# Longer down rounds, one PSUM bank for a gate product, and a new order of work behind the attention

## The chip, the core and the metric

The kernel runs on one core of a Trainium2 chip. The metric is the device time in microseconds (us). A core has five engines that run side by side and wait for each other by semaphores: TensorE (PE) multiplies matrices into PSUM, VectorE (DVE) and ScalarE (ACT) work element by element and empty PSUM, GpSimd (POOL) does small vector work and issues some DMAs, and SyncE (SP) issues most of the other DMAs. Each engine works off its own instructions in a fixed order, so an instruction that waits holds up all those behind it on the same engine.

## The reference

A residual stream of 512 tokens by 1024 features goes through two layers: a gated short convolution with a SwiGLU block behind it, then windowed attention with sinks and again a SwiGLU block. Everything is float32.

```python
def swiglu(h, w_gate_up, w_down):
    g, u = jnp.split(h @ w_gate_up, 2, axis=-1)
    return (jax.nn.silu(g) * u) @ w_down          # F = 2816 hidden columns

mix = short_conv_mixer(rmsnorm(h, a_pre_norm[l]), ...)           # layer 0
h = h + rmsnorm(mix, a_post_norm[l])
h = h + rmsnorm(swiglu(rmsnorm(h, ffn_pre_norm[0]), ...), ffn_post_norm[0])
attn = sliding_window_sink_attention(q, k_sh, v_sh, sinks) @ b_w_o[j]   # layer 1
h = h + rmsnorm(attn, b_post_norm[j])
h = h + rmsnorm(swiglu(rmsnorm(h, ffn_pre_norm[1]), ...), ffn_post_norm[1])
```

## The kernel before

**Three matmuls for one.** Every float32 operand is split into a high part (a copy rounded by ACT: `whi`, `xhi`, `ohi`) and a low part (what is left, subtracted by DVE: `wlo`, `xlo`, `olo`). `mm3` (L190 to L193) then issues three matmuls: high times low, high times high, low times high.

**Seven products for eight.** The large products of a SwiGLU block go by Strassen's scheme: 2 by 2 blocks, seven products P1 to P7 instead of eight. That needs sums of weight blocks. They are made in DRAM: class `Sums` lists DMA copies and accumulating DMAs (`hsum`), `sum_on` begins them at places that the table `BEGIN` names and moves them on a step at each place, and `issue` (L535 in the trace) has POOL issue them. An accumulating DMA waits, on POOL, for the copy that it adds to. Where a sum is not made in DRAM, DVE adds the two blocks (L454).

**SwiGLU.** The 2816 hidden columns are 22 tiles of 128. `gate_jobs` makes two hidden tiles (a pair of "row tiles", index `e`) for gate and up at once: seven jobs, one for each product, each 24 matmuls of 256 columns. The products add up along three chains of PSUM banks, X (P1, P6, P7, P4), Z (P5, P3) and Y (P2); `take(p, e)` empties or combines what stands in a bank behind each product, before the next product is added on top. The result is split by `pair_sums` into the factors of the down product, six small steps that are put off ("late") and worked off one for each later job. `ROUNDS` says which hidden tiles form a round of the down product. `down_jobs` makes seven jobs where a round has four tiles, and eleven where it has six; a job brings one 128x1024 weight tile, is prepared three jobs ahead (`LINE_LEAD`) and its products end with DVE (L636) or, in the first round, ACT (L634) adding PSUM to `mix`. The last four tiles are not a round: `close` or the end of the kernel multiplies them directly.

**The seam.** `close` ends a block: for four row tiles of tokens it makes the last part of the product in two halves, `take` (L259) adds it to `mix`, `square_mix` (L264) squares it, `mean` (L293 on DVE, then L297 on POOL, a power of -0.5) makes the norm's factor, `update` (L302) adds to the stream `h`, `square` (L310), `mean2` (L315, then L319 on POOL) and `norm` (L324) make `xn` for the next block. PE then turns `xn` (`turn`, L335): the turn of tokens' tiles 0 and 1 stands on PE between two parts of the last half product, and the last ones among the first gate products. `Ahead.one` splits one weight tile for the next block (L408 on ACT, L413 on DVE). The attention before it is written as a pipeline of ten steps `i` over eight pairs of heads; the string `ORDER` sets what is issued in a step, all engines in one order.

What a pass of the attention's loop and the seam behind it did (`KT` is 8):

```python
                if op in "RH":
                    issue(len(issues) // 2 if op == "R" else len(issues))
            sum_on(f"a{i + 1}")
        ...
        close(rest_w, at, EARLY, res, ahead)
```

Of the kernel before, what the change touches and what calls it, by code (L numbers as in the profile page):

```python
# [12 lines left out]
AF = mybir.ActivationFunctionType  # L13
# [5 lines left out]
S = 512  # L19
KT = D // P  # L20
F = 2816
NF = F // P
ROUNDS = [(0, 6), (6, 10), (10, 14), (14, 18), (18, 22)]

PLAIN = 2

# [1 line left out]

BEGIN = {
# [4 lines left out]
}  # L34


# [8 lines left out]

EARLY_IN, REST_IN = 2, 0
ORDER = (
    "R- T0 g0 S0 O- T1 Q0 M0 Q1 Z0 P0 P1 S1 T2 L0 Q2 L1 G M1 E00 E01 T3 H- Q3 P2 P3 E10 E11 Z1 z0 K W0 L2 L3 N0 W1 W2 N1 W3 g1 z1"
)
STEP = {  # L50
    "S": "scores", "M": "maxima", "E": "exponents", "N": "normalise", "T": "turn", "P": "high",
# [21 lines left out]
def yoco_kernel(  # L73
# [780 lines left out]
        if square:  # L854
            res.square(t)

    def close(ws, x, k0, res, ahead, then=None):


        n = len(x) - k0  # L860

        def part(ps, t, half, ks):
            unit(ps, t, ws[len(ws) // 2 * half :], x, ks, n, k0)

        begun = [bank("pmix", ps_mm) for _ in range(2)]
        for half in range(2):
            part(begun[half], 0, half, range(n - 1))
            ahead.one()
            ahead.one()
        for t in range(NB):  # L870
            for half in range(2):
                if t == 0:
                    ps = begun[half]
                    part(ps, t, half, range(n - 1, n))
                else:
                    ps = bank("pmix", ps_mm)
                    if (t, half) == (NB - 1, 1):
# [74 lines left out]
    def ffn(l, before, ahead, gain, gpres, following):  # L952
# [20 lines left out]
        def gate_jobs(q, factors, out, to, then):  # L973

            sums = sums_of[f"g{l}{q}"]
            a21, a22, a11, a12 = (Raw(b) for b in sums.blocks)
            s1, s3, *rest = (Raw(b) for b in sums.sums)
            raws = {1: [a11], 2: [a12], 5: [s1], 7: [s3], 4: [a22]}  # L980
            if rest:
                raws[6], raws[3] = ([r] for r in rest)
            else:
                raws[6], raws[3] = [a11, s1], [a12, a11]
            chain = {1: "X", 6: "X", 7: "X", 4: "X", 5: "Z", 3: "Z", 2: "Y"}
            pools = {"X": ps_mm, "Y": ps_pt, "Z": ps_sc}
# [8 lines left out]
            def take(p, e):  # L995
                x, y, z = (banks[c][e][:, :256] if c in banks else None for c in "XYZ")
                gr = kept[2]
                g0, g1 = (gr[:, c : c + 256] for c in (e * S, e * S + 256))
                s, u = kept[e][:, :256], kept[e][:, 256:]
                if p in (1, 6):  # L1000
                    nc.scalar.activation(s, x, AF.Copy)  # L1001
                elif p == 2:
                    nc.vector.tensor_tensor(out=g0, in0=y, in1=s, op=ALU.add)
                elif p == 5:
                    nc.scalar.activation(u, z, AF.Copy)
                elif p == 7:
                    nc.vector.tensor_tensor(out=u, in0=x, in1=u, op=ALU.add)
                elif p == 3:
                    nc.vector.tensor_tensor(out=g1, in0=z, in1=s, op=ALU.add)
                else:  # L1010
                    for g, m in ((g0, x), (g1, u)):
                        nc.vector.scalar_tensor_tensor(out=g, in0=m, scalar=-1.0, in1=g,
                                                       op0=ALU.mult, op1=ALU.mult)

            def run(p):
                def products(job):
                    if not kept:
                        kept.extend([slot("st"), slot("st"), wide("gr")])
                    whi, wlo = split[p] if p in split else job.w
                    c = chain[p]  # L1020
                    opened = c not in banks
                    if opened:
                        banks[c] = [bank("g" + c.lower(), pools[c]) for _ in range(2)]
                    for e in range(2):
                        for k in range(4):
                            kk = slice(e * S + k * P, e * S + (k + 1) * P)
                            mm3(banks[c][e][:, :256], whi[:, kk], wlo[:, kk], *factors[p][k],
                                opened and k == 0, k == 3 and p in (2, 3, 4),
                                skip_group_check=True)
                        take(p, e)  # L1030
                return products

            def gate():
                for e in range(2):
                    both = kept[2][:, e * S : (e + 1) * S]
                    nc.scalar.activation(both, both, AF.Silu)

# [407 lines left out]
    with tc.manual_schedule(engines=ALL):  # L1445
        sum_on("a0")
        for i in range(KT + 2):
            for c in ORDER.split():
                if c == "K":
                    if i == 2:  # L1450
                        ks.append(rope_split(rope(pk[1], nc.gpsimd), nc.gpsimd))
                    continue
                late = c.endswith("-")
                op, n = c[0], [int(d) for d in c[1:].rstrip("-")]
                t = i - late
                if op == "g":

                    u = 2 * (t - EARLY - 1) + n[0]
                    if u in (-2, -1, 2, 3):
                        j = u + 2 if u < 0 else u  # L1460
                        early_w.append(split_weights(w_o[j // 2, j % 2], slots=j >= EARLY_IN))
                    continue
                if op in "SMENTPLWO":
                    t -= op in "TPLWO"
                    of = hp
                elif op in "QRH":
                    t += LEAD
                    of = qs
                elif op == "G":
                    t += LEAD + 1  # L1470
                    of = qs
                    if KT <= t < KT + 4:
                        j = t - KT
                        rest_w.append(split_weights(w_o[j // 2, 2 + j % 2], slots=j >= REST_IN))
                else:
                    t = 2 * (t - EARLY - 1) + n.pop(0)
                    of = early
                if 0 <= t < len(of) and not (op in "RH" and t < LEAD - 1):
                    getattr(of[t], STEP[op])(*n)
                if op in "RH":  # L1480
                    issue(len(issues) // 2 if op == "R" else len(issues))
            sum_on(f"a{i + 1}")

        res = Update(mix_o, B_ATT, [G_FPRE[1]])
        res.leaves = True
        res.load()
        ahead = Ahead(first_weights(1))
        close(rest_w, at, EARLY, res, ahead)
    ffn(1, res, ahead, B_FFN[1], [], [])


# [93 lines left out]
```

## Time and profile before

| | |
|---|---|
| time, median of 3 runs | 1027.85 us (1027.74, 1027.85, 1031.52) |
| the profiled execution: its time | 1032.36 us |
| its span, first to last instruction | 1030.6 us |
| granted TensorE clock over the span | 0.997 |
| busy: PE, weight loads, DVE, ACT, POOL | 1019.1, 927.8, 823.2, 577.7, 195.3 us |
| the conv seam (layer 0) | about 160 to 190 us into the span |
| attention, and the seam behind it | about 540 to 660, and 660 to 700 us |

PE is busy in almost every slice, so a saving counts only where PE waits. Time that an engine spends issuing or waiting isn't busy time. In the views, a wait stands in brackets behind the instruction that waited, with what ended it; "x4" is four instructions in one row, and a row with a count gives the time of all of them together.

### The profile page before, as it was taken

How to read it: one execution, taken by the hardware profiler on the slowest of the kernel's cores; microseconds unless marked ns; L12 is line 12 of the kernel's file. 1: busy time of each engine (PE TensorE's matmuls, PEld its weight loads, DVE VectorE, ACT ScalarE, POOL GpSimd, SP SyncE). 2: the span in 40 equal slices, each digit the busy share in tenths (PEclk: the TensorE clock that was granted, in tenths of full speed). 3: DMA queues.
4: the chain of work that ended last, by engine and by line, in shares of the span. 5: the costliest groups of instructions: out<-in, count | busy, mean ns of one | idle time of the engine just before them, and what ended most of it. 6: DMA issues, size and time to landing. Idle time of an engine off the chain costs nothing.

```text
span 1030.6 us, 17465 instructions
## 1 busy us (share of the span) xinstructions
PE 1019.1 (99%) x6648; PEld 927.8 (90%) x6648; DVE 823.2 (80%) x1400; ACT 577.7 (56%) x1035; POOL 195.3 (19%) x259
## 2 busy tenths in 40 slices
PE   9999999999999999999999999989999999999997
PEld 8888888999899898998897888879998999989986
DVE  5766767888688879779869999668886788887786
ACT  7323445865655354656566677667565554645642
POOL 0333033111111111000124653121111010210001
PEclk9999999999999999999999999999999999999999
DMA  9897689459968699778404789865889676988732
GB/s 355 284 261 229 184 254 353 130 169 299 351 229 293 194 314 332 242 232 296 146 21 149 190 273 254 248 223 158 261 287 328 176 252 203 312 296 251 246 136 82
DMA packets 66580, 244.59 MB, mean 237 GB/s; under 512 B 7872, under 2 KB 8384, under 8 KB 54720
## 3 DMA queue, kind: packets, MB, share of 16 engines
q1 hardware_dynamic: 51328, 145.98, 38.4%
q0 software_dynamic: 14592, 96.48, 36.4%
q8 instruction: 52, 0.85, 0.3%
q10 hardware_dynamic: 576, 1.02, 0.3%
q14 instruction: 32, 0.26, 0.1%
HBM read 237.15 MB, written 102.76 MB: 330 GB/s over the span
## 4 chain that ended last, share of the span: by engine, by line
PE 90%; DVE 4%; DMA 3%; ACT 1%; issue 1%; POOL 1%; DVEq 0%; ACTq 0%
PE gx L193 7%; PE gx L192 7%; PE gx L191 7%; PE gz L193 4%; PE gz L192 4%; PE gz L191 4%; PE pcub L192 4%; PE pcub L193 4%; PE pcub L191 4%; PE px L191 4%; PE px L192 4%; PE px L193 4%; PE pmix L192 2%; PE pmix L191 2%; PE pmix L193 2%; DMA hsum<-in_w_gb_dram 2%
## 5 line engine op out<-in xcount | busy, mean ns | idle before, releaser
L467 DVE TENSOR_TENSOR wlo<-raw,whi 128x1024 fp32r<-128x1024 f32 x225 | 275.2, 1227 | 93.3 <-ACT whi L466 93.2
L466 ACT ACTIVATE whi<-raw 128x1024 fp32r<-128x1024 f32 x225 | 234.2, 1049 | 117.5 <-DVE raw L454 20.4
L191 PE MATMUL gx<-xt,whi 128*128 128x256 f32 x480 | 135.8, 283 | 0.0
L192 PE MATMUL gx<-xt,whi 128*128 128x256 f32 x480 | 135.8, 283 | 0.0
L193 PE MATMUL gx<-xt,wlo 128*128 128x256 f32 x480 | 135.8, 283 | 0.0
L191 PEld LDWEIGHTS gx<-xt,whi 128*128 128x128 f32 x480 | 92.2, 192 | 0.0
L192 PEld LDWEIGHTS gx<-xt,whi 128*128 128x128 f32 x480 | 92.2, 192 | 0.0
L193 PEld LDWEIGHTS gx<-xt,wlo 128*128 128x128 f32 x480 | 92.2, 192 | 0.0
L535 POOL DMA_DIRECT2D hsum<-in_w_gb_dram x96 | 63.4, 747 | 143.7 <-ACT whi L466 82.2
L1001 ACT ACTIVATE st<-gx 128x256 f32<-128x256 f32 x80 | 30.6, 385 | 83.5 <-PE gx L193 83.5
L535 POOL DMA_DIRECT2D hsum<-hsum x32 | 25.3, 790 | 262.4 <-ACT whi L466 208.6
L192 PE MATMUL pcub<-xhi,whi 128*128 128x512 f32 x168 | 65.4, 389 | 0.0
L191 PE MATMUL pcub<-xlo,whi 128*128 128x512 f32 x168 | 65.4, 389 | 0.0
L193 PE MATMUL pcub<-xhi,wlo 128*128 128x512 f32 x168 | 65.4, 389 | 0.0
L191 PE MATMUL px<-wlo,ahi 128*128 128x512 f32 x120 | 46.7, 389 | 0.0
L192 PE MATMUL px<-whi,ahi 128*128 128x512 f32 x120 | 46.7, 389 | 0.0
L193 PE MATMUL px<-whi,alo 128*128 128x512 f32 x120 | 46.7, 389 | 0.0
L193 PE MATMUL gx<-xhi,wlo 128*128 128x256 f32 x160 | 45.3, 283 | 0.0
L191 PE MATMUL gy<-xlo,whi 128*128 128x256 f32 x160 | 45.3, 283 | 0.0
L192 PE MATMUL gy<-xhi,whi 128*128 128x256 f32 x160 | 45.3, 283 | 0.0
L193 PE MATMUL gy<-xhi,wlo 128*128 128x256 f32 x160 | 45.3, 283 | 0.0
L191 PE MATMUL gz<-xt,whi 128*128 128x256 f32 x160 | 45.3, 283 | 0.0
(268 smaller groups left out, 3122.5 us busy)
## 6 DMA issues: line engine op xcount, KB each, us to landing
hsum<-in_w_gb_dram POOLq DMA_DIRECT2D x96, 512.0 KB, 7.9
raw<-hsum SPq DMA_DIRECT2D x88, 512.0 KB, 8.2
raw<-in_w_gb_dram SPq DMA_DIRECT2D x60, 512.0 KB, 7.4
hsum<-in_w_dn_dram POOLq DMA_DIRECT2D x36, 512.0 KB, 8.3
raw<-in_w_dn_dram SPq DMA_DIRECT2D x32, 512.0 KB, 7.3
hsum<-hsum POOLq DMA_DIRECT2D x28, 512.0 KB, 5.6
raw<-in_w_in_dram SPq DMA_DIRECT2D x21, 512.0 KB, 7.6
hsum<-in_w_dn_dram POOLq DMA_DIRECT2D x12, 768.0 KB, 12.6
```

The lines of the kernel that those rows point to most:

```text
L191: nc.tensor.matmul(out, whi, xlo, start=start, stop=False, **kw)
L192: nc.tensor.matmul(out, whi, xhi, start=False, stop=False, **kw)
L193: nc.tensor.matmul(out, wlo, xhi, start=False, stop=stop, **kw)
L466: self.begun = nc.scalar.activation(hi[:, :n], raw, AF.Copy)
L467: nc.vector.tensor_tensor(out=lo[:, :n], in0=raw, in1=hi[:, :n].bitcast(F32), op=ALU.subtract)
L535: nc.gpsimd.dma_start(dst, src, max_dma_last_dim=4 * 4 * S, **kw))
L1001: nc.scalar.activation(s, x, AF.Copy)
```

## The change

Three edits.

1. `ROUNDS` has three rounds of six tiles and a last group of four, in place of one round of six, three of four and the four. Each layer has one round fewer; the sums for a round of six are 768 KB to a DMA in place of 512 KB. `BEGIN` follows: `d03` and `d13` are gone, `g09` and `g19` begin at `0p4` and `1p4`.
2. A gate product's two row tiles share one PSUM bank (256 columns each), and `take` runs once behind both, on 512 columns, in place of once behind each on 256.
3. The seam behind the attention. Three of the four `ahead.one()` go into the attention's step `i == KT`, in front of the last `weigh` steps. `res` and `res.load()` are made a little earlier. In the last step (`i == KT + 1`) POOL issues nothing more; the summing of `a10` runs inside `close`, behind row tile 0 (as it already does in the conv seam).

```diff
-ROUNDS = [(0, 6), (6, 10), (10, 14), (14, 18), (18, 22)]
+ROUNDS = [(0, 6), (6, 12), (12, 18), (18, 22)]
...
-    def close(ws, x, k0, res, ahead, then=None):
+    def close(ws, x, k0, res, ahead, then=None, each=2):
...
-            ahead.one()
-            ahead.one()
+            for _ in range(each if half == 0 or each > 1 else 0):
+                ahead.one()
...
                     if opened:
-                        banks[c] = [bank("g" + c.lower(), pools[c]) for _ in range(2)]
+                        banks[c] = bank("g" + c.lower(), pools[c])
                     for e in range(2):
                         for k in range(4):
                             kk = slice(e * S + k * P, e * S + (k + 1) * P)
-                            mm3(banks[c][e][:, :256], whi[:, kk], wlo[:, kk], *factors[p][k],
-                                opened and k == 0, k == 3 and p in (2, 3, 4),
-                                skip_group_check=True)
-                        take(p, e)
+                            mm3(banks[c][:, e * 256 : (e + 1) * 256], whi[:, kk], wlo[:, kk],
+                                *factors[p][k], opened and e == k == 0,
+                                e == 1 and k == 3 and p in (2, 3, 4), skip_group_check=True)
+                    take(p)
...
             def gate():
-                for e in range(2):
-                    both = kept[2][:, e * S : (e + 1) * S]
-                    nc.scalar.activation(both, both, AF.Silu)
+                nc.scalar.activation(kept[2], kept[2], AF.Silu)
...
         for i in range(KT + 2):
+            if i == KT:
+                res = Update(mix_o, B_ATT, [G_FPRE[1]])
+                res.leaves = True
+                ahead = Ahead(first_weights(1))
+            if i == KT + 1:
+                res.load()
             for c in ORDER.split():
+                if c == "A":
+                    if i == KT:
+                        ahead.one()
+                    continue
...
-                if op in "RH":
+                if op in "RH" and i <= KT:
                     issue(len(issues) // 2 if op == "R" else len(issues))
-            sum_on(f"a{i + 1}")
-
-        res = Update(mix_o, B_ATT, [G_FPRE[1]])
-        res.leaves = True
-        res.load()
-        ahead = Ahead(first_weights(1))
-        close(rest_w, at, EARLY, res, ahead)
+            if i <= KT:
+                sum_on(f"a{i + 1}")
+        close(rest_w, at, EARLY, res, ahead, lambda: sum_on(f"a{KT + 2}"), 1)
```

In `ORDER`, `L2 L3 N0 W1` becomes `L2 L3 A A A N0 W1`. `take` keeps its seven cases.

What moves on POOL at the seam behind the attention. `ur` is the norm's factor (L297 for `mean`, L319 for `mean2`), the `hsum<-in_w_dn` rows are the DMAs of the sum for down round 1 of layer 1 (four copies, then two that add); before:

```order
L535 DMA hsum_187<-in_w_gb_dram 64x2048
L535 DMA hsum_208<-in_w_dn_dram 64x2048
L535 DMA hsum_209<-in_w_dn_dram 64x2048
L535 DMA hsum_210<-in_w_dn_dram 64x2048
L535 DMA hsum_211<-in_w_dn_dram 64x2048
L535 DMA hsum_208<-in_w_dn_dram 64x2048
L535 DMA hsum_209<-in_w_dn_dram 64x2048
L297 TENSOR_TENSOR ur_7503<-uv_7502,mhalf 128x1
L319 TENSOR_TENSOR ur_7503<-uv_7502,mhalf 128x1
```

The same place on POOL in the changed kernel:

```order
L535 DMA hsum_183<-in_w_gb_dram 64x2048
L535 DMA hsum_204<-in_w_dn_dram 96x2048
L535 DMA hsum_205<-in_w_dn_dram 96x2048
L535 DMA hsum_206<-in_w_dn_dram 96x2048
L535 DMA hsum_207<-in_w_dn_dram 96x2048
L297 TENSOR_TENSOR ur_7248<-uv_7247,mhalf 128x1
L535 DMA hsum_204<-in_w_dn_dram 96x2048
L535 DMA hsum_205<-in_w_dn_dram 96x2048
L319 TENSOR_TENSOR ur_7248<-uv_7247,mhalf 128x1
```

The two adding DMAs have moved from in front of row tile 0's first factor (L297) to behind it, and now stand in front of its second (L319); the four copies are half as large again.

What moves on DVE at the same seam, from the last steps of the attention (`plo`, `lp`, `olo`) to the first `take` (L259); before:

```order
L1347 TENSOR_TENSOR plo_7432<-pt_7426,phi_7431 128x512
L1347 TENSOR_TENSOR lp_5860<-pt_7445,lp_5859 128x2x128
L1365 TENSOR_TENSOR olo_7497<-po_7467,ohi_7496 128x512
L413 TENSOR_TENSOR wlo_7523<-raw_7507,whi_7522 128x1024
L413 TENSOR_TENSOR wlo_7529<-raw_7509,whi_7528 128x1024
L413 TENSOR_TENSOR wlo_7544<-raw_7526,whi_7543 128x1024
L413 TENSOR_TENSOR wlo_7550<-raw_7532,whi_7549 128x1024
L259 TENSOR_TENSOR mixo_6963<-pmix_7511,mixo_6963 128x512
```

The same place on DVE in the changed kernel:

```order
L1349 TENSOR_TENSOR plo_7295<-pt_7289,phi_7294 128x512
L1349 TENSOR_TENSOR lp_5716<-pt_7308,lp_5715 128x2x128
L413 TENSOR_TENSOR wlo_7340<-raw_7249,whi_7339 128x1024
L413 TENSOR_TENSOR wlo_7346<-raw_7251,whi_7345 128x1024
L413 TENSOR_TENSOR wlo_7352<-raw_7343,whi_7351 128x1024
L1367 TENSOR_TENSOR olo_7380<-po_7330,ohi_7379 128x512
L413 TENSOR_TENSOR wlo_7395<-raw_7349,whi_7394 128x1024
L259 TENSOR_TENSOR mixo_6819<-pmix_7383,mixo_6819 128x512
```

Three of the four weight splits have moved in front of `olo`, which PE needs for the last quarter of each product of the seam; one is left between `olo` and the first `take`.

The second round of the down product on DVE, layer 0, before (a round of four tiles: one pair of additions to `mix`, L636, behind each split `wlo`):

```order
L467 TENSOR_TENSOR wlo_3543<-raw_3389,whi_3542 128x1024
L636 TENSOR_TENSOR mix_2857<-mix_2857,px_3551 128x512
L636 TENSOR_TENSOR mix_2859<-mix_2859,px_3552 128x512
L467 TENSOR_TENSOR wlo_3568<-raw_3391,whi_3567 128x1024
L636 TENSOR_TENSOR mix_2867<-mix_2867,pz_3574 128x512
L636 TENSOR_TENSOR mix_2869<-mix_2869,pz_3575 128x512
```

The second half of the same round on DVE in the changed kernel, now a round of six, with the late steps of `pair_sums` (L578 to L588):

```order
L636 TENSOR_TENSOR mix_2813<-mix_2813,px_3736 128x512
L636 TENSOR_TENSOR mix_2815<-mix_2815,px_3737 128x512
L636 TENSOR_TENSOR mix_2813<-mix_2813,pz_3757 128x512
L636 TENSOR_TENSOR mix_2815<-mix_2815,pz_3758 128x512
L467 TENSOR_TENSOR wlo_3854<-raw_3693,whi_3853 128x1024
L578 TENSOR_TENSOR a_663_3735<-gr_3480,a_663_3735 128x256
L467 TENSOR_TENSOR wlo_3874<-raw_3731,whi_3873 128x1024
L581 TENSOR_TENSOR s_3733<-gr_3480 128x256
L582 TENSOR_SCALAR s_3733<-s_3733,gr_3480 128x256
L467 TENSOR_TENSOR wlo_3896<-raw_3754,whi_3895 128x512
```

The additions now come in fours with splits between, and the late steps of the gate product ahead stand in the same stretch.

More of the change, by code (lines that the diff above doesn't have):

```diff
@@ L47 @@
 ORDER = (
-    "R- T0 g0 S0 O- T1 Q0 M0 Q1 Z0 P0 P1 S1 T2 L0 Q2 L1 G M1 E00 E01 T3 H- Q3 P2 P3 E10 E11 Z1 z0 K W0 L2 L3 N0 W1 W2 N1 W3 g1 z1"
+    "R- T0 g0 S0 O- T1 Q0 M0 Q1 Z0 P0 P1 S1 T2 L0 Q2 L1 G M1 E00 E01 T3 H- Q3 P2 P3 E10 E11 Z1 z0 K W0 L2 L3 A A A N0 W1 W2 N1 W3 g1 z1"
 )
@@ L993, in gate_jobs, with take, tiles @@
             banks, kept = {}, []
[L995 to L999, printed above, removed]
+            def take(p):
+                x, y, z = (banks.get(c) for c in "XYZ")
+                st, u, gr = kept
+                g0, g1 = (gr.rearrange("p (e h c) -> p e h c", e=2, h=2)[:, :, h]
+                          for h in range(2))
+                def tiles(a):
+                    return a.rearrange("p (e c) -> p e c", e=2)
                 if p in (1, 6):
-                    nc.scalar.activation(s, x, AF.Copy)
+                    nc.scalar.activation(st, x, AF.Copy)
                 elif p == 2:
-                    nc.vector.tensor_tensor(out=g0, in0=y, in1=s, op=ALU.add)
+                    nc.vector.tensor_tensor(out=g0, in0=tiles(y), in1=tiles(st), op=ALU.add)
                 elif p == 5:
@@ L1008, in take @@
                 elif p == 3:
-                    nc.vector.tensor_tensor(out=g1, in0=z, in1=s, op=ALU.add)
+                    nc.vector.tensor_tensor(out=g1, in0=tiles(z), in1=tiles(st), op=ALU.add)
                 else:
                     for g, m in ((g0, x), (g1, u)):
-                        nc.vector.scalar_tensor_tensor(out=g, in0=m, scalar=-1.0, in1=g,
+                        nc.vector.scalar_tensor_tensor(out=g, in0=tiles(m), scalar=-1.0, in1=g,
                                                        op0=ALU.mult, op1=ALU.mult)
```

4 rows, old and new, of the table BEGIN are left out of this document.

## The prediction

> **What bounds the kernel now.** I read the page's busy times first, then what PE waited for, then PE's granted clock around the one wait found there, then the engines behind that wait.
>
> ```profile
> PE 1019.1 (99%) x6648; PEld 927.8 (90%) x6648; DVE 823.2 (80%) x1400; ACT 577.7 (56%) x1035; POOL 195.3 (19%) x259
> ...
> PE xt L335 <- ACT xn L324: 2.7, 1, 2.7
> PE idle L663 <- DVE ones L140: 1.1, 1, 1.1
> PE psc L1273 <- DVE nm L1285: 0.6, 2, 0.3
> ...
> 580.00:600.00 20.00, 19.56 (x139) 16.49 (x138) 19.72 (x56) 14.54 (x43) 12.56 (x12) 1.00 0.69 178
> ```
>
> PE is busy for 1019.1 of 1030.6 us. The change alters none of PE's matmuls in number or width, so it can only shorten waits, and of those the list has a single one that isn't tiny: 2.7 us in which PE waits for `xn` of a row tile before it can turn it. The last row is a window (its ends and length, then PE, weight loads, DVE, ACT, POOL busy, PE clock, DMA share, GB/s) with one of the 0.3 us waits in it: the clock stays at 1.00. The 2.7 us lie in the seam behind the attention; the windows there and PE's timeline:
>
> ```profile
> 676.00:680.00 4.00, 4.00 (x19) 3.30 (x19) 2.81 (x7) 3.47 (x7) 1.48 (x2) 1.00 1.01 252
> 680.00:684.00 4.00, 2.22 (x11) 1.54 (x9) 3.26 (x7) 2.79 (x7) 0.55 (x1) 1.00 0.98 321
> 684.00:688.00 4.00, 3.10 (x18) 2.91 (x19) 3.56 (x7) 2.91 (x6) 0.93 (x1) 0.76 0.46 186
> 688.00:692.00 4.00, 4.00 (x26) 3.67 (x25) 2.58 (x7) 3.00 (x7) 0.94 (x2) 0.82 0.14 54
> ...
> 681.95 0.27 PE L335 MATMUL xt<-ident,xn 128*128 128x128 f32 x1
> 684.90 2.39 PE L335 MATMUL xt<-ident,xn 128*128 128x128 f32 x15 [2.69 <-ACT xn L324]
> ```
>
> Behind the wait the granted clock is 0.76 and 0.82 for four us each, which costs 4 x 0.24 + 4 x 0.18 = 1.7 us. All that can be won at this place is 2.7 + 1.7 = 4.4 us.
>
> Why `xn` is late is told by POOL, DVE and ACT:
>
> ```profile
> 659.93 2.29 POOL L535 DMA_DIRECT2D hsum<-in_w_dn_dram  x4
> 671.22 0.80 POOL L535 DMA_DIRECT2D hsum<-in_w_dn_dram  x1 [9.00 <-DMA hsum<-in_w_dn_dram]
> 673.02 0.79 POOL L535 DMA_DIRECT2D hsum<-in_w_dn_dram  x1 [1.00 <-DMA hsum<-in_w_dn_dram]
> 673.56 0.85 POOL L297 TENSOR_TENSOR ur<-uv,mhalf 128x1 f32<-128x1 f32 x1
> 677.24 0.56 POOL L319 TENSOR_TENSOR ur<-uv,mhalf 128x1 f32<-128x1 f32 x1 [2.83 <-DVE uv L315]
> 678.81 0.93 POOL L297 TENSOR_TENSOR ur<-uv,mhalf 128x1 f32<-128x1 f32 x1 [1.02 <-DVE uv L293]
> ...
> 662.35 0.69 DVE L1365 TENSOR_TENSOR olo<-po,ohi 128x512 fp32r<-128x512 f32 x1 [3.98 <-ACT ohi L1364]
> 663.30 4.63 DVE L413 TENSOR_TENSOR wlo<-raw,whi 128x1024 fp32r<-128x1024 f32 x4 [0.26 <-ACT whi L408]
> 667.85 1.28 DVE L259 TENSOR_TENSOR mixo<-pmix,mixo 128x512 f32<-128x512 f32 x2
> 670.08 0.21 DVE L293 TENSOR_SCALAR uv<-us 128x1 f32<-128x1 f32 x1
> 674.45 1.28 DVE L302 SCALAR_TENSOR_TENSOR h<-mixo,ur,h 128x1024 f32<-128x1024 f32 x1 [3.56 <-POOL ur L297]
> ```
>
> Row tile 0's mean stands ready at 670.3 (L293), but POOL can't take it: it waits, for 9.00 and 1.00 us, for two copies issued at 659.93 to land before it may issue the DMAs that add to them. L297 comes at 673.56, some 3 us late, and DVE's update (L302) idles 3.56 us. Row tile 1 follows behind it on DVE: its L297 is at 678.81, and PE goes on 6.1 us later. The DVE rows show a second, smaller delay: four splits (L413) stand ahead of the first `take`, after DVE idled 3.98 us.
>
> **Part 1, the rounds of six.** Matmuls: none more or fewer. DVE does 14 additions fewer in each layer, 28 in all:
>
> ```profile
> L467 DVE TENSOR_TENSOR wlo<-raw,whi 128x1024 fp32r<-128x1024 f32 x223 | 273.8, 1232 | 93.3 <-ACT whi L466 93.2
> L466 ACT ACTIVATE whi<-raw 128x1024 fp32r<-128x1024 f32 x223 | 232.9, 1053 | 114.9 <-DVE raw L454 20.4 <-PE pcub L192 17.5 <-PE px L193 16.8
> L636 DVE TENSOR_TENSOR mix<-mix,px 128x512 f32<-128x512 f32 x54 | 36.0, 686 | 5.6 <-PE px L193 5.2
> L588 DVE TENSOR_TENSOR alo<-s,ahi 128x512 fp32r<-128x512 f32 x40 | 27.4, 686 | 0.1
> L582 DVE SCALAR_TENSOR_TENSOR s<-s,gr 128x256 f32<-128x256 f32 x36 | 15.2, 422 | 0.6
> L1009 DVE TENSOR_TENSOR gr<-gz,st 128x256 f32<-128x256 f32 x40 | 15.2, 417 | 2.0 <-PE gz L193 2.0
> 220.00:240.00 20.00, 20.00 (x169) 20.00 (x168) 17.23 (x28) 11.91 (x20) 3.98 (x6) 1.00 0.60 157
> 480.00:500.00 20.00, 20.00 (x90) 16.55 (x89) 19.74 (x27) 7.21 (x10) 0.22 (x1) 1.00 0.80 256
> ```
>
> That is 28 x 0.686 = 19 us of DVE, all beside PE: in 480 to 500, in the last of the old rounds, DVE was busy for 19.74 of 20.00 us and PE for all 20.00. So it is worth nothing in time. It costs one job more in each layer (33 for 32, but three half wide where one was), also hidden. The cover is the three-job lead; what can use it up is a rival below. SP issues 14 DMAs more, in halves of the same bytes; POOL 16 fewer, each half as large again. In the down rounds and the gates nothing on the list waits for a DMA.
>
> **Part 2, one bank.** Each gate product's work behind it falls from two instructions of 417 ns to one of 686 ns (the 512-wide row above), so DVE gains some 0.15 us on each of three, and about as much on each of the last product's two pairs: at most 0.8 us for a gate and 16 us over 20 gates, hidden like the rest. What it adds: `take` waits for both halves, so a chain's bank comes free later than its first half did. Between two products of chain X there stands another product (24 matmuls, 2.8 us at the gates' pace of 169 in 20 us), and one `take` needs 0.7. Nothing on PE's path: 0.
>
> **Part 3, the seam.** Three splits go into the 3.98 us that DVE idled ahead of `olo`: 3 x 1.2 = 3.6 us, so `olo` moves by some tenths, and PE has other quarters of the product to do meanwhile. One split is left ahead of the first `take`, which can come up to 3 of the 4.63 us earlier, if PE has its product ready. The weight fetches that SP issues behind those splits start earlier too, by up to 4 us (663.30 less the idle time's start, 662.35 - 3.98), and run beside the copies. POOL now reaches L297 of row tile 0 with no wait ahead of it. But the wait itself isn't gone: the two adding DMAs stand behind L297 and ahead of L319, so L319 of tile 0 and L297 of tile 1 queue behind them, and the copies that they wait for are now 768 KB.
>
> When do the copies land? The page has two sizes of this very DMA, and the conv seam shows the new POOL order (two adds, four copies, L319, L297):
>
> ```profile
> hsum<-in_w_dn_dram POOLq DMA_DIRECT2D x36, 512.0 KB, 8.3
> hsum<-in_w_dn_dram POOLq DMA_DIRECT2D x12, 768.0 KB, 12.6
> ...
> 163.70 0.95 POOL L297 TENSOR_TENSOR ur<-uv,mhalf 128x1 f32<-128x1 f32 x1 [16.46 <-DVE uv L293]
> 164.61 1.66 POOL L535 DMA_DIRECT2D hsum<-in_w_gb_dram  x2
> 165.72 2.57 POOL L535 DMA_DIRECT2D hsum<-in_w_dn_dram  x4
> 168.13 0.99 POOL L319 TENSOR_TENSOR ur<-uv,mhalf 128x1 f32<-128x1 f32 x1
> 169.12 0.92 POOL L297 TENSOR_TENSOR ur<-uv,mhalf 128x1 f32<-128x1 f32 x1
> 176.62 1.91 PE L335 MATMUL xt<-ident,xn 128*128 128x128 f32 x16
> ```
>
> There the adds don't wait, L297 of tile 1 is at 169.12, 7.5 us ahead of the turn, and PE doesn't stop. Behind the attention the turn is due at 681.95 and takes `xn` 6.1 us after L297, so L297 of tile 1 must come by 675.9; it came at 678.81.
>
> Low end: the copies land as now, second add at 673.0, L319 half a us later, L297 one more (168.13 to 169.12): 674.6, no wait, 4.4 us won. High end: 12.6 / 8.3 = 1.52 times the 13.1 us from 659.93 to 673.02, that is 679.8, L297 at 681.3, 2.5 later than now: 2.5 lost. Between: the adds came 1.8 us apart, so one copy passes in 1.8 us; half a copy more for the two ahead gives 674.8, for all four sharing alike 676.6. I take 676.0, nearer the second, since the DMA share in these windows is 0.98 to 1.01; L297 then at 677.5, 1.3 earlier than now, and PE's wait 1.4 in place of 2.7. The clock: waits of 0.3 us on the list are followed by a full clock, one of 2.7 isn't; for 1.4 the bounds are 0 and 1.7 us, and I take no loss.
>
> The Trainium skill, "TensorE: Matmul & The Clock Gate", section "What's actually happening", puts the drop of the clock behind an idle window of about 3.4 us. By it the sum would have no clock loss to win here, 1.3 in place of 3.0; this trace shows a drop behind 2.7 us, and the measurement decides.
>
> **The sum.** 0 + 0 + 1.3 + 1.7 = 3.0 us, against the profiled execution's own 1032.36: 1029.4. The median of the timed runs is 1027.85, 4.5 below that execution, and one of the three runs was at 1031.52. The gap is just what the wait and its clock cost (4.4), so the quicker runs may well have little of the wait. Nothing here shows them, so the gain on the median lies between 0 and 3.0; I take half, 1.5: **1026.4 us**.
>
> **Rivals.**
> *The wait goes altogether.* The copies land about as now and the timed runs had the whole wait: 1027.85 - 4.4 = 1023.4. For it: the conv seam has this order and no wait. Against it: there the adds found their copies landed. The rows of 8.3 and 12.6 us are 4.3 apart. By the fit in the Trainium skill's "DMA: Bandwidth & Descriptors", section "Anatomy of one DMA — SWDGE (gpsimd) path" (2.0 us and 1 us for each 436 KB), an estimate is 0.6 us for the larger copy, which would leave no wait; the rows here say more.
> *POOL's adds hold up the seam more than before* (the other side). If the second add issues later than 677.3, L297 of tile 1 comes later than 678.81. At the high end 2.5 us are lost: 1030.4; and where the timed runs had no wait, up to 2.7 + 2.5 + 1.7 = 6.9: 1034.8. For it: DMA is saturated and SP's fetches start earlier. Against it: the adds now have until L319 is due, 3.7 us later than L297 (673.56 to 677.24). The same page of the Trainium skill, section "SWDGE vs HWDGE vs iDMA", has each DMA engine serve POOL's and SP's queues in turn. By that rule fetches that start 4 us earlier take half of those, 2 us, from the copies: add at 678.0, 0.7 us slower than now.
> *DVE falls behind in the second round of six.* In the last six jobs it has six splits (7.4 us), ten additions (6.9) and six late steps (some 4.2: three of 686 ns, five of about 420), 18.5 us beside 5.5 jobs of PE, 5.5 x 12 / 90 x 20 = 14.7. It decides once DVE is later than the lead allows, about 3 us (two jobs, 5.3, less one split on ACT and one on DVE, 2.3). 3.8 - 3 = 0.8 us in the second round of each layer, the third having no late steps: 1026.4 + 1.6 = 1028.0, with more if it enters late. Against it: the first round has nearly this load and no wait, and five quiet jobs come first.
> *It does nothing*: the timed runs had no wait, 1027.8.
>
> **How the numbers follow.** Smaller wait, 1025.0 to 1027.4: 0.42. Wait gone: 0.20. Adds later: 0.16. DVE behind: 0.08. Nothing: 0.14. Half a per cent, about what can be told from no change here, is 5.1 us: below 1022.7 or above 1033.0. Faster takes under half of the second case, 0.08; slower the far part of the third and some of the fourth, 0.07; within 0.85. The range runs from 1022.8 to 1031.0: it leaves out the fastest tail and the upper parts of the third and fourth cases.
>
> **What would show it.** In the new profile: L297 of tile 0 without a wait ahead of it; the adds behind it, waiting for copies; L319 right behind them near 676.5; PE's wait for `xn` about 1.4 us and the clock at 1.00; no PE wait in gates or down rounds while DVE's busy time falls by some 30 to 35 us. I am wrong if PE waits in a down round, if the adds issue after 677, or if the time falls by more than the seam's 4.4 us.

## The result, and the profile after

| | before | after |
|---|---|---|
| time, median | 1027.85 us | 1035.46 us (1034.72 to 1038.41, 5 runs) |
| ratio, with its 95% interval | | 1.0072 (1.0059 to 1.0085) |
| the profiled execution: time, span | 1032.36, 1030.6 us | 1035.4, 1033.6 us |
| busy: PE, DVE, ACT, POOL | 1019.1, 823.2, 577.7, 195.3 us | 1019.1, 800.5, 566.4, 186.5 us |

The change makes the kernel 0.7% slower, outside the range forecast. What PE waited for, in the changed kernel (line, what it waits for: us in total, times, longest):

```profile
PE px L191 <- DVE mix L636: 4.3, 1, 4.3
PE px L191 <- ACT mix L634: 1.3, 1, 1.3
```

Besides these there are only the two tiny waits of before (1.1 us, and 0.6 in two pieces), which every run below has too. The wait for `xn` at the seam, 2.7 us before, is gone. In its place stand two waits for a PSUM bank (`px`) of the down product. PE's timeline has both, and windows of 10 us give the place and the clock (columns as in the prediction):

```profile
274.15 0.50 PE L191 MATMUL px<-wlo,ahi 128*128 128x512 f32 x1 [1.28 <-ACT mix L634]
...
295.04 0.50 PE L191 MATMUL px<-wlo,ahi 128*128 128x512 f32 x1 [4.26 <-DVE mix L636]
```

```profile
270.00:280.00 10.00, 8.72 (x39) 6.90 (x38) 5.91 (x5) 6.92 (x9) 3.46 (x5) 1.00 1.07 344
...
290.00:300.00 10.00, 5.74 (x19) 4.25 (x18) 8.88 (x14) 4.73 (x6) 0.00 (x0) 0.83 0.92 376
```

Both lie in the first down round of layer 0, which has six tiles in both kernels. The clock of 0.83 over 10 us costs 1.7 us. Together 1.3 + 4.3 + 1.7 = 7.3 us, nearly all of the 7.6 us between the medians.

PE waits for a bank that ACT or DVE has yet to empty; but these engines were late themselves. ACT, then DVE, of the changed kernel in that stretch:

```profile
264.48 1.06 ACT L466 ACTIVATE whi<-raw 128x1024 fp32r<-128x1024 f32 x1 [0.84 <-DMA raw<-hsum]
271.29 1.06 ACT L466 ACTIVATE whi<-raw 128x1024 fp32r<-128x1024 f32 x1 [5.75 <-DMA raw<-hsum]
272.56 1.06 ACT L466 ACTIVATE whi<-raw 128x1024 fp32r<-128x1024 f32 x1 [0.21 <-DMA raw<-in_w_dn_dram]
273.52 1.07 ACT L634 ACTIVATE mix<-px 128x512 f32<-128x512 f32 x2
...
290.00 1.06 ACT L466 ACTIVATE whi<-raw 128x1024 fp32r<-128x1024 f32 x1 [6.86 <-DMA raw<-hsum]
```

```profile
291.09 1.22 DVE L467 TENSOR_TENSOR wlo<-raw,whi 128x1024 fp32r<-128x1024 f32 x1 [6.21 <-ACT whi L466]
...
294.30 1.28 DVE L636 TENSOR_TENSOR mix<-mix,px 128x512 f32<-128x512 f32 x2
```

ACT can't split a weight tile because its fetch from a sum in DRAM (`raw<-hsum`) hasn't landed: it idles 5.75 and 6.86 us. DVE's split idles 6.21 us for ACT's, and the addition that empties `px` (L636) stands behind that split on DVE, until 294.30. A late DMA stops ACT, then DVE, then PE. SP didn't issue the fetches late: those up to 262 us start at 250.27 to 261.25 us, before at 250.53 to 261.56. They landed late, 16.6 us (median) after their issue, before 11.5. Later issues of SP are late as well (one of 267.18 comes at 271.25).

The DMAs of the 45 us from 250 to 295, first before, then after (queue 0 carries POOL's sums, queue 1 SP's fetches: packets, MB, share of 16 engines; then issues: KB each, median us to landing):

```profile
q1 hardware_dynamic: 3476, 8.30, 47.6%
q0 software_dynamic: 880, 5.77, 45.7%
...
hsum<-in_w_dn_dram POOLq DMA_DIRECT2D x6, 512.0 KB, 7.6
raw<-hsum SPq DMA_DIRECT2D x5, 512.0 KB, 11.1
```

```profile
q0 software_dynamic: 1088, 7.40, 58.4%
q1 hardware_dynamic: 3350, 7.28, 44.3%
...
hsum<-in_w_dn_dram POOLq DMA_DIRECT2D x6, 768.0 KB, 11.3
raw<-hsum SPq DMA_DIRECT2D x5, 512.0 KB, 17.1
```

Ahead of the first round and beside it, the sum for down round 2 (`d02`; counted from 0, so the third) is made, now with 768 KB to a DMA. POOL's queue moves 1.63 MB more, SP's 1.02 MB less, and a weight takes 17.1 us to land in place of 11.1. How full the engines were here could be read before, too; windows of before, then of after:

```profile
240.00:260.00 20.00, 20.00 (x169) 20.00 (x168) 17.22 (x28) 11.91 (x20) 4.03 (x7) 1.00 0.97 329
260.00:280.00 20.00, 20.00 (x110) 17.41 (x110) 12.96 (x18) 11.41 (x15) 3.56 (x6) 1.00 1.05 350
```

```profile
240.00:260.00 20.00, 20.00 (x169) 20.00 (x168) 16.99 (x22) 11.30 (x16) 4.22 (x7) 1.00 1.02 324
260.00:280.00 20.00, 18.72 (x102) 15.95 (x101) 12.58 (x14) 10.12 (x13) 3.46 (x5) 1.00 1.04 356
```

Before, the DMA share (the last column but one; it adds up the time of packets, so it can pass 1) was 0.97 and 1.05 for 40 us with PE at full rate. The engines were full, though nothing on PE's list said so. But a full share doesn't tell by itself how near a stall is. The changed kernel is as full ahead of and in the first down round of layer 1, and PE doesn't wait there:

```profile
760.00:780.00 20.00, 20.00 (x160) 19.63 (x159) 15.82 (x21) 11.28 (x15) 2.44 (x3) 1.00 1.03 282
780.00:800.00 20.00, 20.00 (x90) 16.58 (x89) 11.90 (x14) 11.90 (x17) 2.66 (x4) 1.00 1.04 346
```

The time to landing tells more: there, from 765 to 810 us, the `raw<-hsum` fetches of 512 KB land after 12.0 us, not 17.1.

### The profile page after: what moved, and what is told of

The parts are those of the page before. It is cut to its first block, busy times and chain, and to the rows that moved or that the text cites. A ratio compares the mean times of both kernels' runs of the same rounds, so it can differ in the third digit from the quotient of the medians.

```text
span 1033.6 us, 17235 instructions
## 1 busy us (share of the span) xinstructions
PE 1019.1 (99%) x6648; PEld 927.2 (90%) x6648; DVE 800.5 (77%) x1274; ACT 566.4 (55%) x957; POOL 186.5 (18%) x243
## 3 DMA queue, kind: packets, MB, share of 16 engines
q10 hardware_dynamic: 576, 1.02, 0.3%
## 4 chain that ended last, share of the span: by engine, by line
PE 89%; DVE 4%; DMA 4%; ACT 1%; issue 1%; DVEq 0%; SPq 0%; ACTq 0%
PE gx L193 7%; PE gx L192 7%; PE gx L191 7%; PE pcub L192 4%; PE pcub L193 4%; PE pcub L191 4%; DMA raw<-hsum 4%; PE gz L193 4%; PE gz L191 4%; PE gz L192 4%; PE px L191 3%; PE px L193 3%; PE px L192 3%; PE pmix L193 3%; PE pmix L192 3%; PE pmix L191 3%
## 5 line engine op out<-in xcount | busy, mean ns | idle before, releaser
L1005 ACT ACTIVATE st<-gx 128x512 f32<-128x512 f32 x40 | 23.9, 598 | 89.6 <-PE gx L193 89.5
L535 POOL DMA_DIRECT2D hsum<-hsum x28 | 22.3, 798 | 243.0 <-ACT whi L466 207.0
L297 POOL TENSOR_TENSOR ur<-uv,mhalf 128x1 f32<-128x1 f32 x15 | 13.8, 922 | 217.0 <-DVE uv L293 216.8
L191 PE MATMUL gz<-xlo,whi 128*128 128x256 f32 x160 | 45.3, 283 | 0.0
L191 PE MATMUL gz<-xt,whi 128*128 128x256 f32 x160 | 45.3, 283 | 0.0
L192 PE MATMUL gx<-xhi,whi 128*128 128x256 f32 x160 | 45.3, 283 | 0.0
L192 PE MATMUL gz<-xt,whi 128*128 128x256 f32 x160 | 45.3, 283 | 0.0
```

Of the source, the lines that this page charges most:

```text
L191: nc.tensor.matmul(out, whi, xlo, start=start, stop=False, **kw)
L192: nc.tensor.matmul(out, whi, xhi, start=False, stop=False, **kw)
L297: nc.gpsimd.tensor_tensor(out=self.r[:, t : t + 1], in0=self.v[:, t : t + 1], in1=mhalf[:, :1], op=ALU.pow)
L535: nc.gpsimd.dma_start(dst, src, max_dma_last_dim=4 * 4 * S, **kw))
L1005: nc.scalar.activation(st, x, AF.Copy)
```

## The experiments

Theory A: the longer sums fill the DMA engines ahead of the first down round of layer 0, so its weights land late. Its rivals are named in the expectations. The medians beside the kernel before, on the same chip:

| kernel | median, us | before, us | ratio (95%) |
|---|---|---|---|
| rounds_only | 1038.6 | 1027.94 | 1.0117 (1.0085 to 1.0148) |
| old_rounds | 1028.12 | 1027.94 | 0.9999 (0.9990 to 1.0009) |
| seam_only | 1027.95 | 1027.94 | 0.9997 (0.9988 to 1.0007) |
| d02_later | 1034.47 | 1027.94 | 1.0060 (1.0044 to 1.0076) |
| copies_added | 1031.43 | 1027.85 | 1.0039 (1.0025 to 1.0053) |
| d02_earlier | 1032.09 | 1027.85 | 1.0040 (1.0025 to 1.0055) |
| layer1_as_layer0 | 1045.24 | 1027.85 | 1.0171 (1.0154 to 1.0188) |
| d02_g09_later | 1027.58 | 1027.85 | 0.9993 (0.9984 to 1.0003) |
| spread_a | 1027.52 | 1028.02 | 0.9998 (0.9989 to 1.0008) |
| spread_b | 1027.82 | 1028.02 | 0.9994 (0.9981 to 1.0007) |
| rounds_and_seam | 1035.06 | 1028.02 | 1.0073 (1.0058 to 1.0088) |
| all_bytes_added | 1035.46 | 1028.59 | 1.0067 (1.0050 to 1.0084) |

### Which of the three edits

**The rounds alone.** The kernel before with

```diff
-ROUNDS = [(0, 6), (6, 10), (10, 14), (14, 18), (18, 22)]
+ROUNDS = [(0, 6), (6, 12), (12, 18), (18, 22)]
```

and the new `BEGIN`.

> The kernel before with the rounds of six and their table of beginnings alone; two banks for a gate product and the old seam. Theory A (the longer sums of 768 KB fill the DMA engines ahead of the first down round of layer 0, so that its weights land late): the whole loss is here, PE waits of about 1.3 and 4.3 us in 265 to 300 us and a slower clock for some 3.4 us behind them, together 7.3 us: 1027.85 + 7.3 = about 1035.1, between 1034 and 1036.5. Rival B (the one-bank gates make the splits, and so the fetches, come later): no such waits, 1027 to 1028.5. Rival C (both are needed): about 1030, with only the shorter of the two waits.

1038.6 us, more than the 1034 to 1036.5 expected; the profiled execution, at 1036.29, is the fastest of its four runs, and no trace shows what the others spent. The waits of PE, and the window behind the attention:

```profile
PE px L191 <- DVE wlo L467: 2.3, 1, 2.3
PE xt L335 <- ACT xn L324: 2.1, 1, 2.1
PE px L191 <- DVE mix L636: 1.6, 1, 1.6
```

```profile
688.00:692.00 4.00, 1.94 (x18) 1.65 (x16) 2.96 (x5) 3.33 (x8) 1.48 (x2) 1.00 0.98 242
```

The loss is there with the rounds alone. In this profile the old seam waits as well, 2.1 us for `xn`. The profiled execution of before had a wait there too, 2.7 us with copies of 512 KB, so the trace alone doesn't put this one down to the longer copies.

**The other two edits.** The changed kernel with the old `ROUNDS` and `BEGIN`:

> The changed kernel with the rounds of six, four, four and four and the old table: one-bank gates and the new seam alone. Theory A: no PE wait in any down round; 1026 to 1028, with 1027.85 if the timed runs of before had no wait at the seam and 1026.4 if they had part of it. Rival B: the waits of 1.3 and 4.3 us stay in 265 to 300 us, about 1035. Rival C: about 1030.

1028.12 us, and no PE wait but the two tiny ones. That is 0.1 above theory A's range, and far from the 1035 of B and the 1030 of C: both fall.

**The seam alone.** The kernel before with the edits of `ORDER`, `close` and the attention's loop:

> The kernel before with the new seam behind the attention alone. All theories: nothing changes in the first layer. If the timed runs of before carried the seam's wait (2.7 us and 1.7 us of clock), up to 4.4 us less: 1023.4. If they had none of it, as the gap of 4.5 us between the profiled execution and the median suggests, 1027.3 to 1028, and the profile shows no wait for xn at the seam. Above 1028.5 the adds behind the first factor would hold up the second.

1027.95 us, a ratio of 0.9997. Its profile has no wait for `xn` and a span of 1026.1 us. The profiled execution of before had 1030.6, of which the seam's wait and its clock are 4.4: without them 1026.2. So at the median before didn't pay for the seam either; there was next to nothing to win. The profiled execution's wait isn't that of the usual run: of the 59 timed runs of before that were taken beside the experiments, 12 are above 1029 us (up to 1033.12); of the 50 runs of the five kernels here that have the new seam and no stall in a round, one is (1029.61). Whether those 12 had the seam's wait, no trace shows.

**Rounds and seam, without the one bank.** `take`, `run` and `gate` as before:

> The changed kernel with two banks for a gate product as before: the rounds of six and the new seam. The rounds alone stood at 1038.6, all three edits at 1035.46. If the seam makes those 3.1 us (in the rounds-alone profile PE waits 2.1 us for xn there, and the copies of 768 KB are the cause), this is at 1035 to 1036 with no wait for xn; if the one-bank gates make them (less for ACT and DVE to do when a late weight lands), 1038 to 1039.

1035.06 us and no wait for `xn`. So beside the rounds of six the new seam is worth some 1038.6 - 1035.06 = 3.5 us, loosely known (medians of four runs each, the first from 1036.29 to 1043.33; the two intervals just overlap), and beside the rounds of four nothing. That fits the expectation that the longer copies made the old seam wait in most runs, but only one run of the rounds alone has a trace. The one bank adds 0.4 to it (1035.46), within the spread of either.

### Where the sums are made

**`d02` later.** In the table `0p1` is the place behind the second gate pair of layer 0, and `0s0` the one behind its first down round. The changed kernel with

```diff
-    "0f1": "g05", "0p0": "g06", "0p1": "d02", "0p2": "g07", "0p3": "g08", "0p4": "g09",
+    "0f1": "g05", "0p0": "g06", "0p2": "g07", "0s0": "d02", "0p3": "g08", "0p4": "g09",
```

> The changed kernel with one name moved in the table: the sum for down round 2 of layer 0 (four copies of 768 KB) begins behind the first down round (0s0) in place of behind the second gate pair (0p1). Theory A1 (these copies, on the DMA engines beside the first round's weights, make them late): both PE waits go, and the clock stays full; 1035.46 - 7.3 = 1028.2, between 1027 and 1029. A2 (the longer sum for round 1, begun at the conv seam, left a backlog that lasts to the first down round): the waits stay, 1034 to 1036. Part of each: 1029 to 1033.

1034.47 us. Both A1 and A2 missed what it shows, the waits and two places in windows:

```profile
PE px L191 <- DVE mix L636: 5.2, 2, 3.3
```

```profile
260.00:280.00 20.00, 20.00 (x108) 17.33 (x107) 12.47 (x14) 11.45 (x15) 1.82 (x3) 1.00 0.93 305
280.00:300.00 20.00, 20.00 (x117) 17.74 (x116) 17.39 (x24) 11.53 (x16) 2.03 (x3) 1.00 0.41 127
...
360.00:380.00 20.00, 18.04 (x80) 14.59 (x79) 12.67 (x16) 7.64 (x9) 3.18 (x4) 1.00 1.04 295
380.00:400.00 20.00, 16.73 (x111) 15.24 (x110) 15.19 (x22) 9.07 (x12) 1.54 (x2) 0.91 0.83 263
```

The first round runs without a stop, as A1 says, and the stall has moved to the second round, where the changed kernel had none: `d02`'s last add (issued at 338 us) and those for `g08` now stand close ahead of the four copies of `g09` (344 to 350 us), ahead of that round. That these are the cause is so far argued; the next run tests it.

**`g09` later too.** As above, and `"0p4": "g09"` becomes `"0s1": "g09"`.

> The changed kernel with d02 at 0s0 (as in the run before, where the first round's waits went and two of 3.3 and 1.9 us came in the second round) and g09 moved from 0p4, just ahead of that second round, to 0s1 behind it. Theory A: no wait in either round, 1027.5 to 1028.8. If the second round's waits stay (1033.5 to 1035), they came from the adds for d02 or from g08, not from g09's four copies. Between: 1029 to 1033.

1027.58 us, no wait in any round. Here part of the weights of `g09` is fetched ahead of the last additions to it, so the last gate pair works with sums that aren't whole; all transfers run, but those fetches don't wait for the additions. In `spread_a` and `spread_b` below every sum is whole before it is read.

**`d02` earlier.** The changed kernel with layer 0's table made like layer 1's, `"0f0": "g05", "0f1": "g06", "0p0": "d02"`:

> The changed kernel with layer 0's table made like layer 1's: g05 at 0f0, g06 at 0f1, d02 at 0p0, one place earlier each, so that the four copies of 768 KB run in the second gate pair, where the DMA share was 0.53 to 0.65, and only one pair of adds is left for the third. Theory A (too much at one place): both PE waits go; 1035.46 - 7.3 = 1028.2, the time of before, and no second down round stalls (the places behind 0p2 are those of the changed kernel, where it had no wait). Rival E (a round of six needs more than the DMA engines can give wherever its sum is made): a wait of some us stays in one of the three rounds, 1031 to 1036.

1032.09 us, not as A expected but within what E did. PE waits once, for 2.6 us, still in the first round, and the clock drops behind it:

```profile
260.00:270.00 10.00, 7.43 (x51) 6.58 (x50) 3.88 (x5) 2.80 (x4) 0.00 (x0) 1.00 1.02 307
270.00:280.00 10.00, 10.00 (x39) 8.05 (x38) 6.12 (x8) 7.12 (x10) 2.31 (x4) 0.83 1.06 303
```

2.6 + 1.7 = 4.3 on top of 1027.85 is 1032.15. An earlier start didn't help enough, since the DMA share was then 1.02 from 220 to 240 already: a backlog is handed on from one place to the next. `spread_b` below keeps `d02` at this place with only `g05` ahead of it in the block, and the wait is gone.

**Layer 1 like layer 0.** The changed kernel with `"1f1": "g15", "1p0": "g16", "1p1": "d12"`:

> The changed kernel with layer 1's table made like layer 0's: g15 at 1f1, g16 at 1p0, d12 at 1p1, one place later each; layer 0 as it was, with its 7.3 us. Theory A: the same stall a second time, in 770 to 810 us: 1035.46 + 7.3 = about 1042.8, between 1039 and 1045. Rival E, or a cause that layer 0 alone has (the backlog of the conv seam): layer 1 stays without a wait, 1034 to 1036.5.

1045.24 us, 9.8 more than the changed kernel and just above the 1039 to 1045 expected. Its waits:

```profile
PE px L191 <- ACT mix L634: 6.9, 2, 6.6
PE px L191 <- DVE mix L636: 5.8, 1, 5.8
```

The 5.8 us (and 0.3 of the 6.9) are in layer 0, the 6.6 in layer 1's first round, which hadn't stalled. So the cause is not special to layer 0; what kept layer 1 free of it was one line of the table.

**Spread.** The changed kernel with, in `spread_a`,

```diff
-    "0f1": "g05", "0p0": "g06", "0p1": "d02", "0p2": "g07", "0p3": "g08", "0p4": "g09",
+    "0f1": "g05", "0p0": "g06", "0p2": "g08", "0s0": "d02", "0p3": "g07", "0p5": "g09",
```

and in `spread_b` with `"0p0": "d02"` and `"0s0": "g06"` in place of `"0p0": "g06"` and `"0s0": "d02"`.

> The changed kernel with layer 0's sums begun at g08 0p2, d02 0s0, g07 0p3, g09 0p5, so that neither the gate pair ahead of the first nor that ahead of the second down round holds four copies; every sum is whole before it is read. Theory A (a backlog on the DMA engines that runs into a down round): no PE wait in a down round, 1027.0 to 1028.8. If g09's copies, which now run beside the second round, or d02's adds still fill the engines there, a wait in 350 to 395 us and 1030 to 1034. Rival E: a wait in one of the rounds wherever the sums begin.

> As spread_a, but with d02 at 0p0 and g06 at 0s0: the four copies of 768 KB in the second gate pair, as in d02_earlier (2.6 us of waiting and a slower clock in the first round), but without g06's four copies and two adds ahead of them and beside them. Theory A, with the backlog carried on from one place to the next: some 2 MB less to copy and 1 MB less to add ahead of the first round, so no wait there, 1027.0 to 1028.8. If the wait of 2.6 us stays, 1032, it is d02's size alone and not the backlog.

1027.52 and 1027.82 us, no PE wait in a round, the time of the kernel before. The first round in `spread_a`, then in `spread_b`:

```profile
260.00:280.00 20.00, 20.00 (x108) 17.36 (x108) 12.65 (x14) 11.45 (x15) 2.82 (x5) 1.00 0.95 314
```

```profile
260.00:280.00 20.00, 20.00 (x108) 17.37 (x107) 12.53 (x14) 11.53 (x15) 2.85 (x5) 1.00 1.03 337
```

`spread_b` is as full here as the changed kernel (1.03 for 1.04). What tells the runs apart is the landing of the weights issued from 250 to 262 us: its median is 8.1 to 14.5 us in the runs without a wait in this round (`spread_b` 14.5), and 15.1 to 17.7 us in all those with one. The rounds of six are not slow in themselves, rival E falls. And with the stall out, all three edits together are worth nothing that can be told (0.9998, 0.9989 to 1.0008): no version tried beats the kernel before.

### The bytes by themselves

**1 MB more to copy.** The kernel before, rounds of four, with two copies that nobody reads:

```diff
+        if at == "0p1":
+            block = sums_of["d02"].blocks[0]
+            issues.extend([(hbm.tile([2, P, S], F32, name=name("hsum")), block, None)
+                           for _ in range(2)])
```

> The kernel before, rounds of four and all, with one thing added: at 0p1, behind the four copies of 512 KB for d02, two more copies of 512 KB into DRAM that nobody reads. So 1 MB more to copy at the place where the rounds of six bring 1 MB more, and neither a longer round nor a new wait for data. Theory A (bytes on the DMA engines just ahead of the first down round): PE waits in 265 to 300 us, the time rises by 3 to 8 us, 1031 to 1036. Rival D (it is not the bytes but the longer rounds' own order of jobs, splits and late steps): no wait, 1027.5 to 1028.5.

1031.43 us, and PE waits in the same round as in the changed kernel, for the same two engines (the added lines make L636 L640 here, and L634 L638):

```profile
PE px L191 <- DVE mix L640: 1.1, 1, 1.1
...
PE px L191 <- ACT mix L638: 0.9, 1, 0.9
```

Rival D falls: bytes alone stall an unchanged round. But it is only half of the loss.

**All of the bytes.** As above, and further DMAs of 512 KB for the longer `d01` and for the adds: two copies at `o1`, one add each at `0f0`, `0p0` and `0p2`.

> The kernel before, rounds of four, with DMAs of 512 KB added whose results nobody reads, so that the bytes ahead of and in the first down round come to those of the rounds of six: two copies at o1 (for d01), an add at 0f0, an add at 0p0, two copies at 0p1 (for d02), an add at 0p2. With the two copies at 0p1 alone the time was 1031.43, half of the change's loss. Theory A: the rest is the backlog and the adds, and the whole loss is here, PE waits near 1.3 and 4.3 us and a slower clock, 1034 to 1037. If it stays at 1031 to 1032.5, part of the loss is not bytes but the longer rounds' order of jobs.

1035.46 us, the changed kernel's own median. Its waits (L644 and L642 are L636 and L634), and its DMAs from 250 to 295 us:

```profile
PE px L191 <- DVE mix L644: 2.4, 1, 2.4
PE px L191 <- ACT mix L642: 2.0, 1, 2.0
```

```profile
q0 software_dynamic: 1147, 7.43, 58.1%
q1 hardware_dynamic: 3329, 7.27, 44.3%
...
raw<-hsum SPq DMA_DIRECT2D x5, 512.0 KB, 17.2
```

The queues move what they move in the changed kernel (7.43 and 7.27 MB for 7.40 and 7.28), a weight lands after 17.2 us for 17.1, and the loss is the same in size, with the old rounds, banks and seam. It is made up a little differently: the waits are 2.0 and 2.4 us, and the clock is 0.83 over 10 us behind each, 2.0 + 2.4 + 2 x 1.7 = 7.8 in its profile, for the 6.9 us between its medians. So the bytes ahead of this round and in it account for all of the loss, as far as the two intervals can tell (1.0050 to 1.0084, and 1.0059 to 1.0085). How it divides between `d01` and `d02` was measured only for `d02`'s copies.

## Why the prediction was wrong

**Part 1 failed, in the sentence "In the down rounds and the gates nothing on the list waits for a DMA."** It was true of before, and was taken for a reserve, so the term of the rounds' DMAs stood at 0 in the sum. The list shows what is late, not what is nearly late. I showed 220 to 240 (0.60) and 480 to 500 (0.80), where DVE was the question. The view of before that gave the second of these rows had another, for the first down round itself, with a DMA share of 0.98, which the prediction leaves out:

```profile
264.00:293.00 29.00, 29.00 (x134) 24.19 (x133) 20.31 (x28) 15.28 (x20) 3.42 (x5) 1.00 0.98 339
```

I had the price as well: 768 KB took 12.6 us where 512 KB took 8.3, and I used it for the seam alone, though `d02` sends the same DMAs ahead of the first down round. From before alone an estimate was at hand: six DMAs of 256 KB more, 1.57 MB, at the 313 GB/s that before moved in 250 to 295 (14.11 MB in 45 us), are 5 us of lateness if nothing gives way. The fetches measured 6.0 us later, PE's waits 5.6. The missing term is 7.3 us, clock included.

**The rest of part 1 held.** PE's matmuls took no longer, the 28 additions left DVE (18.0 us less in the run with the rounds alone, 19 forecast), and the rival of DVE falling behind in the second round of six didn't occur: no PE wait there.

**Part 2 held in time (0), not in size.** DVE's busy time falls by 5.9 us between the seam alone and seam with one bank (823.3 to 817.4), not by up to 16; all told it fell by 22.7, not by 30 to 35. The size was off because two instructions of 256 columns in a row overlap: alone each takes some 417 ns, but a pair is busy for 0.75 us together (the L1009 row of before at 262.06), not 0.83, and the one of 512 columns for 0.69 (L1013 of the changed kernel at 261.84). That is 0.06 us less for a pair, some 6 us for the five pairs of 20 gates.

**Part 3 was right in its mechanism and wrong in its worth.** POOL at the seam of the changed kernel, and PE's turn:

```profile
676.25 0.94 POOL L297 TENSOR_TENSOR ur<-uv,mhalf 128x1 f32<-128x1 f32 x1 [7.20 <-DVE uv L293]
679.25 0.85 POOL L535 DMA_DIRECT2D hsum<-in_w_dn_dram  x1 [2.06 <-DMA hsum<-in_w_dn_dram]
682.36 0.81 POOL L535 DMA_DIRECT2D hsum<-in_w_dn_dram  x1 [2.27 <-DMA hsum<-in_w_dn_dram]
682.91 0.86 POOL L319 TENSOR_TENSOR ur<-uv,mhalf 128x1 f32<-128x1 f32 x1
683.45 0.84 POOL L297 TENSOR_TENSOR ur<-uv,mhalf 128x1 f32<-128x1 f32 x1
```

```profile
689.16 2.16 PE L335 MATMUL xt<-ident,xn 128*128 128x128 f32 x16
```

L297 of tile 0 waits for DVE, not for a DMA; the adds wait behind it. The attention ends 7.2 us later here (its last `olo` is at 669.56, before at 662.35). Less these, the second add is at 675.2 (676.0 forecast), L319 at 675.7 (676.5), L297 of tile 1 at 676.2 (677.5). PE doesn't wait, where 1.4 us were forecast: at this place the rival "the wait goes altogether" came true, because the chain came 0.8 to 1.3 us sooner than taken (L297 follows L319 in 0.5 us, not 1), and PE's turn begins 5.7 us behind that L297, where 6.1 were taken. But the gain was counted from the profiled execution, and I had noted that the timed runs stood 4.5 us below it, just the price of that wait. Half of 3.0 us was then a guess between two readings, and the runs decide for 0 (seam alone 0.9997).

**The rivals.** With the stall out (1027.52 to 1028.12) the change is the rival "it does nothing", 1027.8. The high end of the range took in mishaps at the seam and DVE falling behind in the second round of six. The sign "PE waits in a down round" was named, and it came, but in the first round and for late weights: that had no case of its own. The rule of the Trainium skill's "DMA: Bandwidth & Descriptors", section "SWDGE vs HWDGE vs iDMA", that a DMA engine serves POOL's and SP's queues in turn, was weighed there in the wrong direction alone, SP's fetches slowing POOL's copies. It works both ways, and the trace agrees: as POOL's share of the engines rose from 45.7 to 58.4%, SP's fell from 47.6 to 44.3% and its fetches took 6.0 us longer. The taking of turns itself no run here shows.

## What to carry to other kernels

A resource that nobody waits for may still be full: before giving a DMA queue more bytes, read the DMA share in the windows around every place where the bytes are moved, not only where a wait is seen. A share near 1 says that there is little room, not that a stall will come: PE ran on at 1.03 and 1.04 in layer 1 of the changed kernel. Beside it, the time that the urgent fetches take to land shows what is left: at the first round of layer 0 PE waited in the runs where it was 15 us or more, and in none where it was 14.5 or less. Enlarging a transfer that isn't urgent (a sum for a later round) is paid for by those that are (the weights for this one), and on an engine that works in order one late weight also holds back the emptying of a PSUM bank behind it. And before a wait in a profile is counted as a gain, see whether the median of the timed runs has it: if the profiled execution is longer by just that wait, it probably doesn't.

## What the runs showed of the hardware

The clock's drop doesn't follow from the wait's length alone. PE's timeline has a wait of 1.96 us in `d02_later` (until 363.84) and one of 1.96 us in `all_bytes_added` (until 274.51). Behind the first the granted clock stayed at 1.00, and behind the second it was 0.83 over 10 us (1.7 us lost). In `rounds_only` it stayed at 1.00 behind 2.1 us and was 0.83 behind 2.3. Behind 2.6 us in `d02_earlier` and 4.3 us in the changed kernel it was 0.83 over 10 us, and behind 5.7 us in `rounds_and_seam` 0.66 over 10 us (3.4 us lost). The Trainium skill, "TensorE: Matmul & The Clock Gate", section "What's actually happening", asks for an idle window of about 3.4 us and says that the window runs freely; waits of 2.0 to 2.7 us were enough here, so the measurement differs on the length.
